# Neighbourhood attention: the products with the values, once 128 weight columns for a query group at a time, now 64 weight columns for one head, by key block

## The chip, the cores and the metric

The kernel runs on one core of one Trainium2 chip. The metric is the device time of one execution, in microseconds (us); before the change its median over three runs is 1502.55 us (1501.95 to 1504.43).

## The reference

One encoder layer over 1024 tokens of width 1024: a hybrid token mixer (an mLSTM group and a neighbourhood-attention group), cross-attention into 256 memory tokens, and a gated convolutional FFN, each followed by a layer norm. The change touches the neighbourhood attention alone. The tokens form a grid of 16 rows by 64 columns. Each of 8 heads of width 64 lets a token look at a window of 8 rows by 16 columns:

```python
s = jnp.einsum('bhrqd,bhrkd->bhrqk', qg, k_rows) * (NA_DIM ** -0.5)
s = jnp.where(mask, s + bias, -jnp.inf)
p = jax.nn.softmax(s, axis=-1)
o = jnp.einsum('bhrqk,bhrkd->bhrqd', p, v_rows)
```

`k_rows` and `v_rows` are the 8 grid rows that belong to a query row, `bias` is a learned relative bias, `mask` keeps the 16 columns. What changes is how the last line, the product of the probabilities with the values, is cut into matmuls.

## The kernel before

**Blocks.** `na_gen` (L1136) loops over four head pairs `p` and four column blocks `cb` of 16 query columns; such a pair is called a block here, and there are 16. The keys of a block lie in 32 columns of all 16 grid rows, 512 keys, which `vt` (L1175, three buffers, four loads of 64 KB on SyncE's queue) holds as four key blocks of 128 keys (4 grid rows by 32 columns), each with 128 value columns: 64 of the first head and 64 of the second. The queries of a block form four groups `g` of 4 grid rows. A group holds 64 queries of each head, side by side: 128 columns, the first 64 of head 0, the others of head 1. The groups see the key blocks 0-1, 0-2, 1-3 and 2-3, so 2, 3, 3 and 2 of them, 10 in all.

**A group's steps** (L1181 to L1205): scores `S` on TensorE by three matmuls in float32r (`mm3`, L224 to L226, into one of three "Y" banks of PSUM); VectorE adds bias and mask and takes the extreme (L1189); ScalarE the exponential with its sum (L1191); VectorE the reciprocal and the scaling (L1193, L1194). Then TensorE transposes the probabilities, one 128x128 transpose a key block (L1199, tile `tp`), ScalarE copies them to `PT` (L1201), and TensorE multiplies, in fp32, one matmul a key block:

```python
for b in range(nb):
    anchor[0] = T.matmul(po[:, g, :], vt[:, r0 // 4 + b, :], PT[:, b, :], start=b == 0,
                         stop=b == nb - 1)
```

The weights are all 128 value columns, the moving side all 128 queries, so the 128x128 result in `po` (tile `o`, one bank of the two "X" banks a block) holds each head's values under each head's queries. Only the two squares where the heads agree are used: after the fourth group, ScalarE and VectorE read them and split them into a high and a low part, `X2h` and `X2l` (L1206 to L1211, through `split`, L229 and L230).

**The order.** The program is written down group by group, and a scheduler then orders each engine's instructions by a timeline that it simulates, so what stands next to each other on an engine is not what the code says. `mix` (L30) adds a second product to the stage: `out_a` (L1219), the first half of the mixer's output projection (tile `fill`, bias added on GpSimd at L1094), of which it releases a part whenever the main generator has yielded enough of its total, 128 for 16 blocks of four groups with two yields each. After the last part, the weights of the second half of the projection (`w_mix_out`) are loaded; its matmuls (tile `out`, again L224 to L226) read `X2h` and `X2l` of all four head pairs, so those for the first three can run before the last head pair is done. The bias row `b_xo` of the next stage is scaled on VectorE at L1437.

Some small steps early in the program use only a part of the array: L377 multiplies with a single weight column, L385 transposes into 64 columns, L418 to L420 have one row, L431 transposes from 64 rows.

Of the kernel before, what the change touches and what calls it, by code (L numbers as in the profile page):

```python
# [8 lines left out]
F32 = mybir.dt.float32  # L9
# [4 lines left out]
AF = mybir.ActivationFunctionType  # L14
# [15 lines left out]
def mix(tc, anchor, main, total, fill, ftotal, lag, start=None):  # L30


    done = fdone = 0.0
    anchor[0] = start
    names = []
    more = True
    for cost in main:
        done += cost
        names.append(anchor[0])
        at = names[-1 - lag] if len(names) > lag else None  # L40
        while more and fdone / ftotal < done / total and at is not None:
# [15 lines left out]
def encoder(ctx, tc, I, out):  # L57
    nc = tc.nc
    V, A, G, T, S = nc.vector, nc.scalar, nc.gpsimd, nc.tensor, nc.sync
    anchor = [None]  # L60

    def bcast_row(ap, n, off=0):
# [10 lines left out]

    NB = {"X": 2, "Y": 3, "Z": 1, "tp": 2}
    SET = dict(tk="XXYYYZ", cl="X", xk="X", xv="X", st="X", stb="Y", s="Y", mem="XXYYYZ", cu="XXYYYZ", G="Z", num="Y", o="X", S="Y", xq="X", pv="X", S2="XXYYYZ",
               fill="Z", fill2="ZX", out="XXYYYZ", z="XXYYYZ", mx=["tp"], dn=["tp", "tp", "X", "X", "Y", "Y", "Y", "Z"])
# [151 lines left out]
    def split(hi, lo, src):  # L228
        A.activation(hi, src, AF.Copy)  # L229
        V.tensor_tensor(lo, src, hi.bitcast(F32), OP.subtract)  # L230
# [50 lines left out]
    with ExitStack() as ca:  # L281

        yml = None
        with ExitStack() as cm:
# [258 lines left out]
            with ExitStack() as c2:  # L543
# [12 lines left out]
                with ExitStack() as c1:  # L556
# [111 lines left out]
                    p0, s0 = pow2(ln_bound(lnw, lnb)[1], 12)  # L668
# [271 lines left out]
            wc, cb = {}, {}  # L940
# [160 lines left out]
        yna = tuple(t.rearrange("p (k t) -> p k t", k=4) for t in slot("X2"))  # L1101

        with ExitStack() as cn:
# [4 lines left out]
            o = 0  # L1108
# [23 lines left out]
                e_.memset(b_.bitcast(F32), 0.0)  # L1132
            CB = [0, 8, 24, 32]
            vload = [None]

            def na_gen():  # L1136
                n = 0
                for p in range(4):
                    if p % 2:
                        wide = wide1  # L1140
                    else:
                        wide = vecs.tile([128, D], F32, name="vec1", tag="vec1")[:, :576].rearrange(
                            "p (r c) -> p r c", r=12)
                    S.dma_start(wide, I["na_wide"][p])
                    if p == 0:
                        qr = vecs.tile([128, D], F32, name="vec2", tag="vec2").rearrange("p (r c) -> p r c", c=64)
                        kr = wp.tile([128, WP], F32, name="wraw", tag="wraw", bufs=2)[:, :D].rearrange(
                            "p (r c) -> p r c", c=64)
                    else:
                        qr = nw.tile([128, 16, 64], F32, name="qr", tag="qr", bufs=2)  # L1150
                        kr = nw.tile([128, 16, 64], F32, name="kr", tag="kr", bufs=2)
                    S.dma_start(qr, nqk_d[p].rearrange("p (r c) -> p r c", c=64))
                    S.dma_start(kr, nqk_d[4 + p].rearrange("p (r c) -> p r c", c=64))
                    for cb in range(4):
                        ct = (0, 1, 1, 2)[cb]
                        k0 = CB[cb]
                        if cb != 2:
                            for rt, R, dk0 in ((0, 8, 4), (1, 12, 0), (3, 8, 0)):
                                tb = tabs[ct, rt]
                                x0 = (16, 8, 0)[ct]  # L1160
                                G.tensor_tensor(tb, mo_[ct, R], wide[:, dk0:dk0 + R, x0:x0 + 32], OP.subtract)
# [12 lines left out]
                        (V if n < 2 else G).tensor_tensor(kl, kr[:, :, k0:k0 + 32], kh.bitcast(F32), OP.subtract)  # L1174
                        vt = nw.tile([128, 4, 128], F32, name="vt", tag="vt", bufs=3)  # L1175
                        for g in range(4):
                            vload[0] = S.dma_start(vt[:, g, :],
                                        bass.AP(tensor=nv_d.tensor, offset=nv_d.offset + (g * 256 + k0) * 512 + p * 128,
                                                ap=[[64 * 512, 4], [512, 32], [1, 128]]))
                        po = bank("o").rearrange("p (g t) -> p g t", g=4)  # L1180
                        for g in range(4):  # L1181
                            r0, R, rt = ((0, 8, 0), (0, 12, 1), (4, 12, 1), (8, 8, 3))[g]
                            nk = R * 32
                            ps = bank("S")[:, :nk]
                            mm3(ps, qh[:, g, :], ql[:, g, :], kh[:, r0:r0 + R, :].rearrange("p r c -> p (r c)"),
                                kl[:, r0:r0 + R, :].rearrange("p r c -> p (r c)"), True, True)
                            P = nw.tile([128, 384], F32, name="P", tag="P", bufs=5)
                            mn = nw.tile([128, 2], F32, name="mn", bufs=6)
                            V.tensor_tensor_reduce(P[:, :nk], ps, tabs[ct, rt].rearrange("p r c -> p (r c)"), 1.0, BIG,  # L1189
                                                   OP.add, OP.min, mn[:, 0:1])  # L1190
                            A.activation(P[:, :nk], P[:, :nk], AF.Exp, scale=-1.0, bias=mn[:, 0:1],  # L1191
                                         accum_out=mn[:, 1:2])
                            V.reciprocal(mn[:, 1:2], mn[:, 1:2])  # L1193
                            V.tensor_scalar(P[:, :nk], P[:, :nk], mn[:, 1:2], None, op0=OP.mult)  # L1194
                            yield 1
                            nb = R // 4
                            pt = tbank()
                            for b in range(nb):
                                T.transpose(pt[:, b, :], P[:, b * 128:(b + 1) * 128], ident)  # L1199
                            PT = nw.tile([128, 3, 128], F32, name="PT", tag="PT", bufs=3)  # L1200
                            A.activation(PT[:, :nb, :], pt[:, :nb, :], AF.Copy)  # L1201
                            for b in range(nb):
                                anchor[0] = T.matmul(po[:, g, :], vt[:, r0 // 4 + b, :], PT[:, b, :], start=b == 0,
                                                     stop=b == nb - 1)
                            yield 1  # L1205
                        for h in range(2):  # L1206
                            hs = slice(h * 64, h * 64 + 64)
                            src = po[hs, :, h * 64:h * 64 + 64].rearrange("p g (r c) -> p g r c", c=16)
                            oh, ol = (y[hs, p, :].rearrange("p (g r c) -> p g r c", r=4, c=64)
                                      [:, :, :, cb * 16:cb * 16 + 16] for y in yna)  # L1210
                            split(oh, ol, src)  # L1211
# [13 lines left out]
            oa = out_a()  # L1225
            S.dma_start(bmo, bcast_row(I["b_mix_out"], D))
            for _ in range(5):
                next(oa)
            mix(tc, anchor, na_gen(), 128.0, oa, 15.0, 1)

# [704 lines left out]
```

## Time and profile before

| what | value |
|---|---|
| median of three runs | 1502.55 us |
| the profiled execution | 1502.08 us |
| its span, first to last instruction | 1500.0 us |
| mean granted TensorE clock | 0.992 |
| TensorE busy with matmuls, whole span | 1441.3 us (96%) |
| first and last product with the values | 487.2 and 629.3 us |

A row of a timeline has the start, the duration, the engine, the line, the operation, what it writes and reads, its shape and how many; a wait in brackets is the idle time of the engine ahead of it and what ended it, "issue" meaning that the profile shows nothing that it waited for. PE stands for TensorE's matmuls, PEld for its weight loads, which run beside matmuls. An fp32 matmul leaves two records of each. A matmul's record begins when it is taken up and lasts until its result is written, so the records of a stream overlap, and a matmul's share of the engine is read from the distance of starts. Idle time of an engine other than the bound costs nothing.

### The profile page before, as it was taken

Reading aid. Unit: us, or ns where it says so; the run is one execution under the profiler, and the core shown is the slowest. Engines: PE = TensorE matmul, PEld = TensorE weight load, DVE = VectorE, ACT = ScalarE, POOL = GpSimd, SP = SyncE. Lnnn points to the kernel's source line nnn. Section 1 sums busy time; section 2 is a strip of 40 time slices with the busy share of each in tenths; the row PEclk is TensorE's granted clock in tenths of the full one; section 3 lists DMA queues with packets and bytes.
Section 4 is the critical chain, followed back from the end, with each engine's and each line's share of the span. In section 5 each row is a group of like instructions: output and inputs, shape, how many; then the busy total and the mean of one; then the engine's idle time right before and its main releaser. Section 6 shows DMA issues by size and latency. Waiting matters only on the chain. (4 is left out here: it accounts for less than half of the span.)

```text
span 1500.0 us, 21659 instructions
## 1 busy us (share of the span) xinstructions
PE 1441.3 (96%) x8060; PEld 867.1 (58%) x8060; DVE 1036.0 (69%) x1945; ACT 825.7 (55%) x1393; POOL 575.1 (38%) x453
## 2 busy tenths in 40 slices
PE   8999999999999898999999799999999999999998
PEld 6998866456766887874444344444444444444444
DVE  7867866545777687488555868887787789707424
ACT  5766565655554666425444777787777767503000
POOL 5452357303325766045112454443444320300543
PEclk9999999999999999999999899999999999999999
DMA  8846653215544633644333233232233336713121
GB/s 308 318 163 215 197 186 129 84 49 151 164 124 156 206 127 127 239 155 71 85 71 100 88 138 126 113 126 113 113 118 119 143 114 239 271 36 99 48 76 59
DMA packets 116383, 208.61 MB, mean 139 GB/s; under 512 B 40627, under 2 KB 69555, under 8 KB 112950
## 3 DMA queue, kind: packets, MB, share of 16 engines
q1 hardware_dynamic: 115984, 206.47, 41.3%
q8 instruction: 63, 1.03, 0.3%
q0 software_dynamic: 144, 0.49, 0.2%
q14 instruction: 42, 0.34, 0.1%
q10 hardware_dynamic: 150, 0.27, 0.0%
HBM read 154.15 MB, written 45.15 MB: 133 GB/s over the span
## 5 line engine op out<-in xcount | busy, mean ns | idle before, releaser
L1527 POOL TENSOR_TENSOR wraw<-ur 128x512 f32<-128x512 f32 x22 | 45.9, 2085 | 207.1 <-issue 192.3
L225 PE MATMUL dn<-wlo,yp 128*128 128x512 f16 (+1 forms) x284 | 105.1, 370 | 0.0
L224 PE MATMUL dn<-whi,yp 128*128 128x512 f16 (+1 forms) x284 | 104.9, 370 | 0.0
L226 PE MATMUL dn<-whi,yp 128*128 128x512 f16 (+1 forms) x284 | 104.4, 370 | 0.0
L1615 DVE SCALAR_TENSOR_TENSOR cbuf<-C,wdw,cbuf 128x1024 f32<-128x1024 f32 x44 | 69.8, 1587 | 35.0 <-ACT cbuf L1614 34.8
L226 PEld LDWEIGHTS <-wlo 128*128 128x128 f16 x540 | 52.8, 98 | 56.5 <-DVE wlo L204 1.3
L225 PEld LDWEIGHTS <-whi 128*128 128x128 f16 x540 | 52.8, 98 | 55.9 <-issue 3.3
L224 PEld LDWEIGHTS <-whi 128*128 128x128 f16 x540 | 52.8, 98 | 53.1 <-ACT whi L203 0.3
L242 POOL TENSOR_TENSOR lnrs<-lnrs,mhalf 128x1 f32<-128x1 f32 x32 | 25.9, 809 | 137.9 <-DVE lnrs L241 132.2
L204 DVE SCALAR_TENSOR_TENSOR wlo<-wraw,us,whi 128x1024 f16<-128x1024 f32 (+1 forms) x48 | 62.5, 1320 | 18.7 <-ACT whi L203 18.7
L1616 DVE SCALAR_TENSOR_TENSOR cbuf<-C,wdw,cbuf 128x1024 f32<-128x1024 f32 x44 | 70.4, 1601 | 0.7
L252 ACT ACTIVATE r<-r,lnrs 128x1024 f32<-128x1024 f32 x19 | 23.6, 1239 | 78.3 <-DVE lnrs L251 78.0
L203 ACT ACTIVATE whi<-wraw,us 128x1024 f16<-128x1024 f32 (+1 forms) x48 | 51.2, 1102 | 16.4 <-DVE us L176 15.5
L225 PEld LDWEIGHTS <-yp 128*128 128x128 f16 x370 | 36.2, 98 | 39.9
L224 PEld LDWEIGHTS <-yp 128*128 128x128 f16 x370 | 36.2, 98 | 39.8
L1614 ACT ACTIVATE cbuf<-C,bdw,wdw 128x1024 f32<-128x1024 f32 x44 | 54.2, 1234 | 9.1 <-DVE C L1652 8.5
L226 PEld LDWEIGHTS <-yp 128*128 128x128 f16 x370 | 36.2, 98 | 39.7
L224 PE MATMUL tk<-whi,Bo 128*128 128x256 f16 (+1 forms) x192 | 52.6, 274 | 2.5 <-DVE stage L204 2.5
L224 PE MATMUL tk<-whi,Be 128*128 128x256 f16 (+1 forms) x192 | 52.6, 274 | 0.7 <-DVE stage L204 0.7
L225 PE MATMUL tk<-wlo,Be 128*128 128x256 f16 (+1 forms) x192 | 52.4, 274 | 0.8 <-DVE wlo L204 0.8
L225 PE MATMUL tk<-wlo,Bo 128*128 128x256 f16 (+1 forms) x192 | 52.5, 274 | 0.0
L226 PE MATMUL tk<-whi,Be 128*128 128x256 f16 (+1 forms) x192 | 52.5, 274 | 0.0
(526 smaller groups left out, 4892.1 us busy)
## 6 DMA issues: line engine op xcount, KB each, us to landing
ur<-in_w_up_dram SPq DMA_DIRECT2D x22, 1024.0 KB
sv<-in_w_down_dram SPq DMA_DIRECT2D x22, 512.0 KB
y<-cbuf SPq DMA_DIRECT2D x22, 512.0 KB
ur<-y SPq DMA_DIRECT2D x11, 1024.0 KB
wraw<-in_w_down_dram SPq DMA_DIRECT2D x22, 512.0 KB
r<-h SPq DMA_DIRECT2D x11, 512.0 KB
wraw<-in_w_tok_dram SPq DMA_DIRECT2D x10, 512.0 KB
wr<-in_w_xk_dram SPq DMA_DIRECT2D x8, 512.0 KB
```

Of the source, the lines that this page charges most:

```text
L203: A.activation(hi, src, AF.Copy, scale=s)
L204: return V.scalar_tensor_tensor(lo, src, s, hi, op0=OP.mult, op1=OP.subtract)
L224: T.matmul(ps, lh, rh, start=first, stop=False, skip_group_check=skip)
L225: T.matmul(ps, lh, rl, start=False, stop=False, skip_group_check=skip)
L226: return T.matmul(ps, ll, rh, start=False, stop=last, skip_group_check=skip)
L242: G.tensor_tensor(rs[:, 0:1], rs[:, 0:1], mhalf[:, 0:1], OP.pow)
L252: A.activation(r, r, AF.Identity, scale=rs[:, 0:1], bias=rs[:, 1:2])
L1527: G.tensor_tensor(S1, A21, A22, OP.add)
L1614: A.activation(c, C[:, 1:SEQ + 1], AF.Identity, scale=wdw[:, 1, j:j + 1], bias=bdw[:, j:j + 1])
L1615: V.scalar_tensor_tensor(c, C[:, 0:SEQ], wdw[:, 0, j:j + 1], c, op0=OP.mult, op1=OP.add)
L1616: V.scalar_tensor_tensor(c, C[:, 2:SEQ + 2], wdw[:, 2, j:j + 1], c, op0=OP.mult, op1=OP.add)
```

## The change

- A new generator `pv_gen` makes the products of a block. It goes by key block: key block 0 meets groups 0 and 1, key blocks 1 and 2 three groups each, key block 3 groups 2 and 3 (`BG`). For each it issues two matmuls, one a head: 64 weight columns, the head's, into the head's half of the output partitions, and two or three groups of 64 queries as one moving side of 128 or 192 columns. That is 8 matmuls a block for 10, 128 for 160, and only the squares that are used are computed. The moving columns come to 20480 in both.
- So that the groups of a key block lie evenly spaced, `PT` becomes one tile of ten slots a block (two buffers in place of three single ones), sorted by key block (`GSLOT`).
- The products of a block are held in `late` and are issued during the next block: one key block after each group's copy to `PT`. The last block's products come at the end.
- A group now yields once, and the total that `mix` is given falls from 128 to 64.

```diff
+            GSLOT = (0, 1, 4, 7)
+            BG = ((0, 0, 2), (2, 0, 3), (5, 1, 4), (8, 2, 4))
+
+            def pv_gen(p, cb, vt, PT):
+
+                po = bank("o").rearrange("p (g t) -> p g t", g=4)
+                for b in range(4):
+                    s0, g0, g1 = BG[b]
+                    for h in range(2):
+                        hs = slice(h * 64, h * 64 + 64)
+                        anchor[0] = T.matmul(po[hs, g0:g1, hs], vt[:, b, hs], PT[:, s0:s0 + g1 - g0, hs], start=b == 0,
+                                             stop=b == 3, skip_group_check=True)
+                    yield 1
+                for h in range(2):
+                    hs = slice(h * 64, h * 64 + 64)
+                    src = po[hs, :, hs].rearrange("p g (r c) -> p g r c", c=16)
...
+                    split(oh, ol, src)
...
-                        po = bank("o").rearrange("p (g t) -> p g t", g=4)
+                        PT = nw.tile([128, 10, 128], F32, name="PT", tag="PT", bufs=2)
...
-                            PT = nw.tile([128, 3, 128], F32, name="PT", tag="PT", bufs=3)
-                            A.activation(PT[:, :nb, :], pt[:, :nb, :], AF.Copy)
-                            for b in range(nb):
-                                anchor[0] = T.matmul(po[:, g, :], vt[:, r0 // 4 + b, :], PT[:, b, :], start=b == 0,
-                                                     stop=b == nb - 1)
-                            yield 1
...
+                            A.activation(PT[:, GSLOT[g]:GSLOT[g] + 2 * nb - 1:2], pt[:, :nb, :], AF.Copy)
+                            if late is not None:
+                                next(late)
+                        if late is not None:
+                            run(late)
+                        late = pv_gen(p, cb, vt, PT)
+                yield 0
+                run(late)
...
-            mix(tc, anchor, na_gen(), 128.0, oa, 15.0, 1)
+            mix(tc, anchor, na_gen(), 64.0, oa, 15.0, 1)
```

How the instructions then stand, at three places. First TensorE in the middle of the stage, before: `o` are the products, `tp` the transposes, `S` the scores.

```order
L1203 MATMUL o<-PT,vt 128x128 x3
L1199 MATMUL tp<-ident,P 128x128 x2
L224 MATMUL S<-kh,qsh_5431 128x384
L225 MATMUL S<-kl,qsh_5431 128x384
L226 MATMUL S<-kh,qsl_5432 128x384
L224 MATMUL S<-kh,qsh_5431 128x256
L225 MATMUL S<-kl,qsh_5431 128x256
L226 MATMUL S<-kh,qsl_5432 128x256
L1203 MATMUL o<-PT,vt 128x128 x2
L1199 MATMUL tp<-ident,P 128x128 x3
L1203 MATMUL o<-PT,vt 128x128 x2
L1199 MATMUL tp<-ident,P 128x128 x3
```

And after, about the same place:

```order
L1219 MATMUL tp<-ident,P 128x128 x2
L1145 MATMUL o<-PT,vt 64x3x64 x2
L1219 MATMUL tp<-ident,P 128x128 x3
L1145 MATMUL o<-PT,vt 64x3x64 x2
L1145 MATMUL o<-PT,vt 64x2x64 x2
L224 MATMUL S<-kh,qsh_5431 128x256
L225 MATMUL S<-kl,qsh_5431 128x256
L226 MATMUL S<-kh,qsl_5432 128x256
L1219 MATMUL tp<-ident,P 128x128 x3
L224 MATMUL S<-kh,qsh_5440 128x256
L225 MATMUL S<-kl,qsh_5440 128x256
L226 MATMUL S<-kh,qsl_5441 128x256
```

Before, the stage has 64 stretches of products, one a group; after, the 64 pairs (one a key block) stand in 46 stretches, mostly three a block, the last two key blocks of a block together.

The second place is TensorE at the end of the stage, before (`out` is the second half of the output projection):

```order
L1203 MATMUL o<-PT,vt 128x128 x3
L224 MATMUL out<-whi,X2h 128x512
L225 MATMUL out<-wlo,X2h 128x512
L226 MATMUL out<-whi,X2l 128x512
L224 MATMUL out<-whi,X2h 128x512
L225 MATMUL out<-wlo,X2h 128x512
L226 MATMUL out<-whi,X2l 128x512
L224 MATMUL out<-whi,X2h 128x512
L225 MATMUL out<-wlo,X2h 128x512
L226 MATMUL out<-whi,X2l 128x512
L1203 MATMUL o<-PT,vt 128x128 x2
L224 MATMUL out<-whi,X2h 128x512
```

And after:

```order
L1219 MATMUL tp<-ident,P 128x128 x3
L1145 MATMUL o<-PT,vt 64x3x64 x2
L1145 MATMUL o<-PT,vt 64x2x64 x2
L1219 MATMUL tp<-ident,P 128x128 x3
L1219 MATMUL tp<-ident,P 128x128 x2
L1145 MATMUL o<-PT,vt 64x2x64 x2
L1145 MATMUL o<-PT,vt 64x3x64 x4
L1145 MATMUL o<-PT,vt 64x2x64 x2
L224 MATMUL out<-whi,X2h 128x512
L225 MATMUL out<-wlo,X2h 128x512
L226 MATMUL out<-whi,X2l 128x512
L224 MATMUL out<-whi,X2h 128x512
```

Before, the last product is followed at once by output matmuls of the last head pair, which need its split; after, the last block's eight products stand together behind the last transposes, and nine output matmuls of the first three head pairs come behind them.

The third place is VectorE where it scales `b_xo`, before (`ISA` is the reduction with bias and mask, `mn` its extreme and the reciprocal):

```order
L1193 RECIPROCAL mn<-mn 128x1
L1189 ISA P,mn<-S,tb_1_5434 128x384
L1189 ISA mn 128x1
L230 TENSOR_TENSOR X2l<-o,X2h 64x16x16
L1194 TENSOR_SCALAR P<-P,mn 128x256
L1437 TENSOR_SCALAR vec_7270<-vec_7270 128x1024
L1193 RECIPROCAL mn<-mn 128x1 x2
L1194 TENSOR_SCALAR P<-P,mn 128x256
```

And after, where L1437 has become L1453:

```order
L1209 ISA P,mn<-S,tb_1_5434 128x384
L1209 ISA mn 128x1
L230 TENSOR_TENSOR X2l<-o,X2h 64x16x16
L1213 RECIPROCAL mn<-mn 128x1
L1453 TENSOR_SCALAR vec_7190<-vec_7190 128x1024
L1214 TENSOR_SCALAR P<-P,mn 128x256
L1213 RECIPROCAL mn<-mn 128x1
L230 TENSOR_TENSOR X2l<-o,X2h 64x16x16
```

It stands behind the same reduction, with the softmax of the same groups behind it. On SyncE's queue the loads of `w_mix_out` for the second half stand four value loads later than before. Behind the attention stage the cross-attention is in the same order; in the FFN some 30 short pieces have changed places.

More of the change, by code (lines that the diff above doesn't have):

```diff
@@ L75, in encoder @@
     SET = dict(tk="XXYYYZ", cl="X", xk="X", xv="X", st="X", stb="Y", s="Y", mem="XXYYYZ", cu="XXYYYZ", G="Z", num="Y", o="X", S="Y", xq="X", pv="X", S2="XXYYYZ",
-               fill="Z", fill2="ZX", out="XXYYYZ", z="XXYYYZ", mx=["tp"], dn=["tp", "tp", "X", "X", "Y", "Y", "Y", "Z"])
+               fill="Z", out="XXYYYZ", z="XXYYYZ", mx=["tp"], dn=["tp", "tp", "X", "X", "Y", "Y", "Y", "Z"])
     turn = {}
@@ L1134, in encoder @@
             vload = [None]
+            GSLOT = (0, 1, 4, 7)
[12 more added lines that the diff above has]
+                    src = po[hs, :, hs].rearrange("p g (r c) -> p g r c", c=16)
+                    oh, ol = (y[hs, p, :].rearrange("p (g r c) -> p g r c", r=4, c=64)
+                              [:, :, :, cb * 16:cb * 16 + 16] for y in yna)
+                    split(oh, ol, src)
             def na_gen():
+                late = None
                 n = 0
@@ L1199, in na_gen @@
                                 T.transpose(pt[:, b, :], P[:, b * 128:(b + 1) * 128], ident)
-                            PT = nw.tile([128, 3, 128], F32, name="PT", tag="PT", bufs=3)
-                            A.activation(PT[:, :nb, :], pt[:, :nb, :], AF.Copy)
-                            for b in range(nb):
-                                anchor[0] = T.matmul(po[:, g, :], vt[:, r0 // 4 + b, :], PT[:, b, :], start=b == 0,
-                                                     stop=b == nb - 1)
-                            yield 1
[L1206 to L1211, printed above, removed]
+                            A.activation(PT[:, GSLOT[g]:GSLOT[g] + 2 * nb - 1:2], pt[:, :nb, :], AF.Copy)
[6 more added lines that the diff above has]
+                run(late)
             def ylk(y):
```

## The prediction, on record before the run

> **What bounds the kernel now.** I read the page first, then the windows over the neighbourhood-attention stage, then who waited for whom there, then the instructions one by one. The page says that TensorE is the busy engine of the whole program:
>
> ```profile
> PE 1441.3 (96%) x8060; PEld 867.1 (58%) x8060; DVE 1036.0 (69%) x1945; ACT 825.7 (55%) x1393; POOL 575.1 (38%) x453
> ```
>
> That is an average over stages, so the stage itself decides. The products with the values run from 487 to 629 us. Columns: stretch, its length, busy time of each engine (instructions), granted clock, DMA share, GB/s.
>
> ```profile
> 500.00:510.00 10.00, 5.46 (x29) 5.01 (x28) 6.79 (x21) 3.42 (x11) 5.88 (x6) 0.83 0.44 136
> 510.00:540.00 30.00, 30.00 (x208) 27.82 (x207) 23.60 (x66) 21.47 (x62) 21.92 (x24) 1.00 0.48 154
> 540.00:580.00 40.00, 37.34 (x247) 33.15 (x246) 30.55 (x95) 27.34 (x81) 27.57 (x27) 1.00 0.30 99
> 580.00:610.00 30.00, 24.30 (x150) 21.58 (x149) 25.64 (x63) 19.31 (x51) 14.81 (x12) 0.94 0.53 177
> ```
>
> From 510 to 580 PE is busy 67.3 of 70 us and DVE 54.2: a microsecond more or less of TensorE work there is a microsecond of the stage. The holes are at 500 to 510 and 580 to 610. The waits of PE in 476 to 632, and one of DVE (total, times, longest):
>
> ```profile
> PE S L224 <- DVE mn L1189: 8.8, 6, 4.5
> PE o L1203 <- ACT PT L1201: 2.4, 3, 1.9
> PE out L224 <- ACT X2h L229: 1.3, 1, 1.3
> DVE vec L1437 <- DMA vec<-in_b_xo_dram: 4.6, 1, 4.6
> ```
>
> The longest hole is DVE standing 4.6 us for a bias row of the next stage, with the softmax behind it. The change leaves that instruction where it is (one row later on DVE, behind the same reduction), so this hole stays in my sum. The products themselves wait for their probabilities only 2.4 us in all.
>
> **The products: how many columns.** This is the PE timeline (start, duration, line, tile, times) of one query group with three key blocks:
>
> ```profile
> 514.03 0.28 PE L225 MATMUL S<-kl,qsh 128*128 128x256 f32 x1
> 514.15 0.28 PE L226 MATMUL S<-kh,qsl 128*128 128x256 f32 x1
> 514.27 0.83 PE L1203 MATMUL o<-PT,vt 128*128 128x128 f32 x6
> 514.93 0.38 PE L1199 MATMUL tp<-ident,P 128*128 128x128 f32 x2
> ```
>
> Durations overlap, starts don't: six records of L1203 take 514.93 - 514.27 = 0.66 us, 0.11 each. A product is two records (160 in the program, 320 here), so before they cost 320 x 0.11 = 35.2 us:
>
> ```profile
> L1203 PE MATMUL o<-PT,vt 128*128 128x128 f32 x320 | 48.0, 282 | 2.5 <-ACT PT L1201 2.4
> L1201 ACT ACTIVATE PT<-tp 128x384 f32<-128x384 f32 x32 | 15.3, 480 | 6.7 <-PE tp L1199 6.5
> ```
>
> After, each of the 16 blocks (head pair, column block) has four key blocks with 2, 3, 3 and 2 query groups of 64 columns, for each of two heads: eight matmuls of two records, 128 or 192 columns long. By the row above a record of 128 columns takes 0.11, one of 192 then 0.11 x 1.5 = 0.165. One after the other that is 8 x 0.11 + 8 x 0.165 = 2.2 us a block, 35.2 us in all: nothing is saved, since the columns are the same 20480. A saving exists only where the two heads, which sit in different halves of the array, stream side by side. No row of before has two such matmuls next to each other, so I bound it. Lower end: 35.2. The records stand as head 0 first, head 0 second, head 1 first, head 1 second; the second record of a head needs the same half as its first, so in a lone pair only the two in the middle can overlap: three record times for four. In the order a block mostly makes three unbroken stretches, of one, one and two pairs: 3 x 0.11 + 3 x 0.165 + (3 x 0.165 + 2 x 0.11) = 1.54 us, 24.6 in all, 10.6 saved. If whole pairs overlapped it would be 17.6. I take 10.6: the pair's operands share neither weight columns nor output partitions, and the order of the records forbids more.
>
> **What it adds: the array changes its division.** Everything around these products fills all 128 columns. Before has a few places where a smaller tile stands between full ones, and there the weight loads (PEld) show what happens:
>
> ```profile
> 190.68 0.27 PE L225 MATMUL tk<-wlo,Bo 128*128 128x256 f16 x1
> 190.79 0.27 PE L226 MATMUL tk<-whi,Bo 128*128 128x256 f16 x1
> ```
>
> ```profile
> 190.68 0.10 PEld L226 LDWEIGHTS <-Bo 128*128 128x128 f16 x1
> 190.99 0.14 PEld L431 LDWEIGHTS s<-ident,Mr 64*128 64x128 f32 x1 [0.21 <-issue]
> 191.19 0.10 PEld L224 LDWEIGHTS <-Bo 128*128 128x128 f16 x1
> ```
>
> The last full matmul starts at 190.79 and, at 0.11 each, its columns are through at 190.90; the next load, with nothing to wait for, starts at 190.99: 0.09 us in which the array empties, and the load can't hide behind a matmul as others do. For columns in place of rows there is one place, 32 wide:
>
> ```profile
> 131.33 0.30 PEld L376 LDWEIGHTS s<-lf,triL 128*128 128x128 f32 x2
> 131.67 0.09 PEld L377 LDWEIGHTS s<-lf,ones 128*1 128x1 f32 x2
> 131.87 0.10 PEld L224 LDWEIGHTS <-whi 128*128 128x128 f16 x1
> ```
>
> Loads of L376 are 0.11 apart, the second is in at 131.55, its 32 columns take 0.03; the load of L377 starts at 131.67: 0.09 again. Its two records of 64 columns (0.055 each) are through at 131.78, and the full load behind starts at 131.87: 0.09 on the way back too. The exposed loads: of two L420 loads (64 columns) in 0.19 us each lasts 0.13, so they are 0.06 apart; full ones in fp32 are 0.30 - 0.19 = 0.11 apart.
>
> ```profile
> 176.24 0.30 PEld L419 LDWEIGHTS s<-rows,ones 1*128 1x128 f32 x2
> 176.60 0.19 PEld L420 LDWEIGHTS s<-ones,rows 1*64 1x64 f32 x2
> L420 PEld LDWEIGHTS s<-ones,rows x2: 128/130/131, 176.6 to 176.7; 1*64 1x64 f32 x2
> L419 PEld LDWEIGHTS s<-rows,ones x2: 187/187/187, 176.2 to 176.3; 1*128 1x128 f32 x2
> ```
>
> So a stretch of products costs 0.09 + 0.06 going in and 0.09 + 0.11 coming out, 0.35 us. The changed order has the 64 pairs in 46 unbroken stretches: 46 x 0.35 = 16.1 us. The Trainium skill says the same of such changes (TensorEngine Tiling (Array Packing), Tiling Modes: changing the mode, not just the tile, drains the engine); by that rule, and by the rows alike, it speaks against this change. One row speaks the other way, a transpose into 64 columns with no gap at all:
>
> ```profile
> 144.77 0.10 PEld L226 LDWEIGHTS <-Bo 128*128 128x128 f16 x1
> 144.88 0.11 PEld L385 LDWEIGHTS s<-ident,g_sb 128*64 128x64 f32 x1
> 144.99 0.10 PEld L224 LDWEIGHTS <-Be 128*128 128x128 f16 x1
> ```
>
> It is a transpose and the new products are none, so I lean on L377; but it is the only 64-column row, and I keep it as a rival. The same page (Restrictions) says that column tiling and fp32 transposes exclude each other; by that L385 was never a column tile, and the gap would come.
>
> **The rest, and the sum.** The products now trail their block by one: they no longer follow the copy of their own probabilities, so the 2.4 us of waiting for ACT go (bound: 0 to 2.4; I take all, since a whole block lies between). At the end nine output matmuls now stand between the last products and the first one that needs the X2 split, so 1.3 us go; but all eight last products wait for the last copy, 0.48 by its row: -0.8. Of the 8.8 us in which PE waits for DVE, 4.5 belong to the bias row; of the other 4.3, where DVE is late, a slower PE gives some back: 0 to 4.3, I take 1.0, since 510 to 580 shows hardly any. Copies, softmax, splits and value loads are the same in number and size and run beside PE; GpSimd does the same steps in a slightly other order. The mix's total is halved with the number of yields, so the other product comes at the same pace; the second half of w_mix_out is loaded four value loads later, and 36 instead of 45 output matmuls come ahead of the last product, the rest behind it: the same work, so nothing.
> Sum on PE: -10.6 + 16.1 = +5.5; with -2.4 - 0.8 - 1.0 it is +1.3 us. The profiled execution took 1502.08 (span 1500.0), so 1503.4; the median of the three runs is 0.47 above it: 1503.9. A measurement of this kernel tells 0.2%, 3.0 us, from no change; the forecast is within that.
>
> **The rivals.** Each on the same base, 1502.55.
> - *Gaps, but no overlap* (slower). The heads stream one after the other: 0 saved, 16.1 added, 4.2 given back: +11.9, 1514.5. It decides as soon as overlap saves under 0.35 us a stretch; taken alone it means that the halves don't do what the change asks of them. For it: nothing in before shows two halves at once. Against: nothing forbids it.
> - *Overlap, no gaps* (faster). L385 is right for 64 columns: -10.6 - 2.4 - 0.8 = -13.8, 1488.8. DVE, at 54.2 of 70, would still follow.
> - *Neither*: 2.4 and 0.8 alone, 1499.4.
> - *Whole pairs overlap, with gaps*: -17.6 + 16.1 - 3.2 = -4.7, 1497.9. Against it: two records of a head need the same half. The Trainium skill (TensorE: Matmul & The Clock Gate, Part 3) gives for packed matmuls one duration and about 4 ns for each further tile, which would be this case if it held for two-record products.
>
> **How the numbers follow.** Forecast 0.54, no overlap 0.20, no gaps 0.15, neither 0.07, whole pairs 0.04. The forecast's own range is 1500 to 1508 (waits given back or not, a stretch at 0.30 to 0.36): of it 0.1 is faster by over 3.0 us, 0.55 the same, 0.35 slower. Faster: 0.05 + 0.15 + half of 0.07 + most of 0.04 = 0.27; slower: 0.19 + 0.20 = 0.39; the same: 0.34. The range takes in most of both large rivals: 1490 to 1513.
>
> **What would show it.** Right: in the changed profile the loads of head 0's first record start 0.09 us after the columns of the last full matmul, and those of the full matmul behind likewise; the first record of head 1 starts within 0.02 us of head 0's second; PE's waits for the PT copy are gone; the DVE hole at the bias row is still there. Wrong: head 1's records start a record time (0.11 or 0.165) apart from head 0's second (no overlap), or no gap at the edges of a stretch, or new waits of PE that no term here names.

## The result and the profile after

The changed kernel takes 1491.66 us (median of 4 runs, 1489.96 to 1492.36), the kernel before took 1503.49 beside it (4 runs, 1501.95 to 1505.74). The ratio is 0.9918, 95% interval [0.9901, 0.9936]: faster by 0.8%, where I had forecast no measurable change. The profiled executions took 1502.08 and 1489.96 us, 12.12 apart. Of all executions told here one, of the experiment e7 below, was slow (1860.12 us, the other three of e7 1488.97 to 1489.78); its ratio leaves it out.

The page of after, busy time by engine (share of the span, instructions), in a span of 1488.2 us:

```profile
PE 1434.5 (96%) x7996; PEld 843.5 (57%) x7996; DVE 1032.6 (69%) x1945; ACT 823.8 (55%) x1393; POOL 574.8 (39%) x453
```

PE's share is what it was, and says nothing: it lost 6.8 us of busy time in a span that lost 11.8. The windows of after over the stage answer to those of before:

```profile
500.00:510.00 10.00, 5.23 (x22) 3.93 (x21) 5.61 (x14) 3.86 (x12) 5.98 (x6) 0.83 0.45 146
510.00:540.00 30.00, 30.00 (x192) 23.25 (x192) 22.91 (x71) 21.90 (x64) 22.13 (x24) 1.00 0.47 156
540.00:580.00 40.00, 39.28 (x259) 30.15 (x258) 32.13 (x101) 28.58 (x86) 29.84 (x33) 1.00 0.35 114
580.00:610.00 30.00, 25.50 (x160) 18.30 (x159) 26.18 (x78) 23.14 (x64) 13.18 (x9) 0.94 0.52 171
```

From 510 to 580 PE is busy 69.3 of 70 us by this view, so the product stretches look as dense as the rest. Their cost shows only one level lower. The PE timeline of after around one pair of 128-column products, then one of 192:

```profile
525.40 0.38 PE L1219 MATMUL tp<-ident,P 128*128 128x128 f32 x2
525.71 0.44 PE L1145 MATMUL o<-PT,vt 128*64 128x128 f32 x4
526.08 0.39 PE L225 MATMUL S<-kl,qsh 128*128 128x256 f32 x1
...
527.09 0.55 PE L1145 MATMUL o<-PT,vt 128*64 128x192 f32 x4
527.56 0.44 PE L224 MATMUL S<-kh,qsh 128*128 128x384 f32 x1
```

And its weight loads:

```profile
525.25 0.30 PEld L1219 LDWEIGHTS tp<-ident,P 128*128 128x128 f32 x2
525.71 0.20 PEld L1145 LDWEIGHTS o<-PT,vt 128*64 128x64 f32 x4 [0.17 <-issue]
526.08 0.19 PEld L225 LDWEIGHTS S<-kl,qsh 128*128 128x128 f32 x1 [0.17 <-issue]
```

The second transpose starts 0.11 behind the first, at 525.51, and is through at 525.62; the first half load starts at 525.71: 0.09 us of an empty array, as forecast. The next full load starts at 526.08, so the whole stretch of one pair took 0.37. That number decides: with the load of 64 columns (0.05) and the gap behind (0.09) it leaves 0.23 for the columns, two records of 0.11, where three would need 0.33 and four 0.44. Record by record, to the nanosecond, the trace has

```
525.713  head 0, first record      525.873  head 0, second record
525.720  head 1, first record      525.880  head 1, second record
```

Both records of a head run beside both of the other, 7 ns behind. The 192-column pair says the same: 527.56 - 527.09 = 0.47, against 0.05 + 2 x 0.16 + 0.09 = 0.46.

PE's waits in the stage, after:

```profile
PE fill L224 <- DVE r L1089: 5.6, 2, 4.8
PE S L224 <- DVE mn L1209: 2.5, 5, 0.7
PE tp L1219 <- DVE P L1214: 1.2, 1, 1.2
PE out L224 <- ACT whi L126: 1.1, 1, 1.1
PE out L224 <- DVE r L1091: 1.1, 1, 1.1
PE tp L1219 <- ACT PT L1220: 0.4, 1, 0.4
```

The products don't stand among them any more (before 2.4 for the copies of PT), the output matmuls no longer wait for the X2 split (1.3), the scores wait 2.5 in place of 8.8. The hole at the bias row is there as forecast; only another line of PE (`fill`, 4.8) now stands at its end, and behind the bias row DVE waits for one more transfer:

```profile
DVE vec L1453 <- DMA vec<-in_b_xo_dram: 3.7, 1, 3.7
DVE r L1089 <- DMA r<-h: 2.3, 1, 2.3
```

Where the 12.12 us went: the stage itself (first matmul of `fill` to last of `out`) fell from 195.6 to 186.4, -9.2. It began 0.9 later, the stretch from the last `out` to the first `z` is 0.9 shorter, the part from there to the last matmul 2.7 shorter, and 0.2 lie outside the span. For the stage I took each PE record's columns from the trace and added up the time between them, in us; *edges* are the pauses where the width of the weights changes, *long* the other pauses over 0.45, *short* those under it, *rest* all that is left, the other matmuls above all. The last four columns are experiments told below.

```
                    before   after     e1      e3      e9      e4      e12
products, columns    34.88   18.03   34.44   17.57   17.55   27.15   26.96
edges                 0      15.28    0       6.36    5.50    6.84    5.52
long pauses          20.57   16.53   17.90   23.83   17.19   15.21   13.82
short pauses          5.27    2.54    4.34    5.66    5.27    6.36    6.47
rest                134.86  134.02  134.08  134.02  134.11  134.17  134.24
stage               195.58  186.40  190.76  187.44  179.62  189.73  187.01
```

In the stage, then, the columns gave 16.9 and the edges took back 15.3; the pauses gave 6.8 (4.0 and 2.7). These figures come from one profiled execution of each kernel, and a single hole can differ between two of them by some 2 us that no edit touched (see e11).

### The profile page after: what moved, and what is told of

Read it like the earlier page. It is cut to its first block, busy times and chain, and to the rows that moved or that the text cites. A ratio compares the mean times of both kernels' runs of the same rounds, so it can differ in the third digit from the quotient of the medians.

```text
span 1488.2 us, 21528 instructions
## 1 busy us (share of the span) xinstructions
PE 1434.5 (96%) x7996; PEld 843.5 (57%) x7996; DVE 1032.6 (69%) x1945; ACT 823.8 (55%) x1393; POOL 574.8 (39%) x453
## 5 line engine op out<-in xcount | busy, mean ns | idle before, releaser
L224 PE MATMUL tk<-whi,Bo 128*128 128x256 f16 (+1 forms) x192 | 52.5, 274 | 2.3 <-DVE stage L204 2.3
L226 PE MATMUL tk<-whi,Bo 128*128 128x256 f16 (+1 forms) x192 | 52.5, 274 | 0.0
```

Source lines behind the costliest of these rows:

```text
L224: T.matmul(ps, lh, rh, start=first, stop=False, skip_group_check=skip)
L226: return T.matmul(ps, ll, rh, start=False, stop=last, skip_group_check=skip)
```

## The experiments

All are measured against the kernel before, in the same session on the same chip; kernels of different sessions are best compared by their ratios. The scheduler orders every kernel anew. Where an experiment only holds work back (e6 to e11), 98% or more of TensorE's instructions in the stage stand in the same order as in the kernel it is compared with; where it changes the products (e1 to e4, e12) or the release (e5), less, so there more differs than the edit says. My theory after the result: whole pairs overlap, the gaps cost what I said, and a part of the gain comes from the order of the work and not from the halves. The rivals: the halves give all of it, or the waits decide and neither the columns nor the gaps matter.

**Full width (e1).** The changed loop with all 128 weight columns in one matmul: by key block as in after, again 46 stretches, no halves. Its order is not that of after: set side by side, about a fifth of TensorE's instructions in the stage stand elsewhere.

```
-                    for h in range(2):
-                        hs = slice(h * 64, h * 64 + 64)
-                        anchor[0] = T.matmul(po[:, g0:g1, hs], vt[:, b, hs], PT[:, s0:s0 + g1 - g0, hs], start=b == 0,
-                                             stop=b == 3, skip_group_check=True)
+                    anchor[0] = T.matmul(po[:, g0:g1, :], vt[:, b, :], PT[:, s0:s0 + g1 - g0, :], start=b == 0,
+                                         stop=b == 3, skip_group_check=True)
```

> The changed kernel with full-width products: by key block and in the changed order as after, but one matmul of 128 weight columns and 256 or 384 moving columns instead of two of 64, so no half tiles and no change of the array's division. Theory A (the tiles give little: in the trace of after the products' columns fall from 34.9 to 18.0 us, but 46 stretches pay about 0.33 us each at their edges, 15.3; the rest of the 12 us comes from the order, by fewer waits): about 1.5 us slower than after, near 1493 to 1495, with waits as in after. Rival B (the tiles give the gain): back to before, 1500 to 1504.

Measured: 1495.15 against 1502.85, ratio 0.9951 [0.9933, 0.9968]. Its products take the 34.4 us of before and there are no edges, and yet over half of the gain is there. The stage is 4.8 shorter, 3.6 of it in the pauses. PE's waits of e1, to be set beside the 8.8 + 2.4 + 1.3 of before:

```profile
PE S L224 <- DVE mn L1207: 5.4, 5, 1.8
PE tp L1217 <- DVE P L1212: 4.2, 1, 4.2
PE out L224 <- ACT whi L126: 1.9, 2, 1.2
```

From e1 to after the ratio falls from 0.9951 to 0.9918, about 5 us (3.5 by the medians); the intervals just touch, but the stage says the same (190.8 to 186.4). Of these 4.4 us, the columns less the edges make 1.1 (16.4 against 15.3) and shorter pauses 3.2. Whether the halves or the other order shortened the pauses, no run shows.

**Products of the own block (e2).** The products follow their own probabilities again, in place of standing a block behind in the program.

```
-                            if late is not None:
+                            if g == 0:
+                                late = pv_gen(p, cb, vt, PT)
+                            else:
                                 next(late)
-                        if late is not None:
-                            run(late)
-                        late = pv_gen(p, cb, vt, PT)
-                yield 0
-                run(late)
+                        run(late)
```

> The changed kernel without the delay by a block: the products of a key block are written down right after the groups it needs, in their own block. Theory A (the gain beside the tiles comes from the key-block form and the order, and the scheduler hoists the delayed products to where their probabilities are ready anyway): within 3 us of after, 1489 to 1495. Rival C (the delay is what removes the waits on TensorE): 5 to 8 us slower than after, 1496 to 1500, with TensorE waiting for ScalarE's copies again.

Measured: 1493.81, ratio 0.9944 [0.9927, 0.996]; the interval touches that of after. PE waits for the copies again, less than before:

```profile
PE S L224 <- DVE mn L1209: 8.4, 5, 6.0
...
PE o L1145 <- ACT PT L1220: 1.7, 4, 0.8
```

Theory A came out: the delay is worth 1.7 us of that wait and little else that the runs show. The stage, 187.0, is 0.6 longer than after's, in 48 stretches for 46. What more there is in the profiled execution (1.0 between the last `out` and the first `z`, 1.9 behind) lies where the order is the same, so the trace doesn't put it down to the delay.

**One stretch a block (e3).** All eight products stand together behind the transposes of the next block's second group: 16 stretches in place of 46, which saves 9 us of edges if PE is what counts.

```
-                                T.transpose(pt[:, b, :], P[:, b * 128:(b + 1) * 128], ident)
+                                lt = T.transpose(pt[:, b, :], P[:, b * 128:(b + 1) * 128], ident)
-                            if late is not None:
-                                next(late)
-                        if late is not None:
-                            run(late)
+                            if late is not None and g == 1:
+                                with tc.issue_after(lt.ins):
+                                    run(late)
```

> The changed kernel with all eight products of a block issued together, behind the transposes of the next block's second group: 16 stretches instead of 46. Theory A (each stretch costs 0.33 us of TensorE time on the path): 30 x 0.33 = 9.9 us faster than after if nothing else comes late, 1481 to 1486 with some waiting for VectorE given back. Rival D (the gaps fall into time in which TensorE would wait for the softmax anyway): within 3 us of after.

Measured: 1490.02, ratio 0.9915 [0.99, 0.993], the same as after. Rival D came out. The edges did fall by 8.9; the pauses rose by 10.4. PE's timeline of e3 shows where most of that is:

```profile
592.67 0.44 PE L1219 MATMUL tp<-ident,P 128*128 128x128 f32 x2 [0.17 <-ACT PT L1220]
599.16 0.69 PE L224 MATMUL S<-kh,qsh 128*128 128x384 f32 x1 [6.05 <-DVE mn L1209]
```

The next scores wait 6.05 us for DVE. DVE's own timeline there (the bracket is its idle time and what ended it):

```profile
593.42 1.22 DVE L196 TENSOR_REDUCE sc<-vec 128x1 f32<-128x1024 f32 x1 [1.90 <-DMA vec<-in_ln_w_dram]
594.67 0.43 DVE L230 TENSOR_TENSOR X2l<-o,X2h 64x256 fp32r<-64x256 f32 x1
595.13 1.23 DVE L127 TENSOR_TENSOR wlo<-wraw,whi 128x1024 fp32r<-128x1024 f32 x1
596.27 2.30 DVE L199 SCALAR_TENSOR_TENSOR sc<-sc 128x1 f32<-128x1 f32 x1
598.49 0.15 DVE L1213 RECIPROCAL mn<-mn 128x1 f32<-128x1 f32 x1
598.67 0.42 DVE L1209 CUSTOM_DVE_ANT_0 P<-S,tb 128x256 f32<-128x256 f32 x1
```

VectorE stands 1.90 us for a weight row of the layer norm behind the stage and reduces it (L196); then come the attention's own split (L230), a split of output weights (L127) and the bound that is worked out from the row (L199), while the softmax waits behind in the queue. L199 works on a single column and lasts 2.30 us here. It ends 15 ns behind an operation of GpSimd that was under way when it started:

```profile
596.01 2.54 POOL L127 TENSOR_TENSOR wlo<-wraw,whi 128x1024 fp32r<-128x1024 f32 x1 [4.64 <-ACT whi L126]
```

It is the same in after, e1, e2, e5, e7 and e8: L199 starts beside a GpSimd operation and ends 13 to 18 ns behind it. In before, e4 and e9 to e12 none runs beside it, and it takes 0.14 to 0.15 us. So some 2 us of the hole are GpSimd's. e9 takes the hole up.

**Heads apart (e4).** As e3, but the four products of head 0 and then the four of head 1: few neighbours in different halves.

```
-                for b in range(4):
-                    s0, g0, g1 = BG[b]
-                    for h in range(2):
-                        hs = slice(h * 64, h * 64 + 64)
+                for h in range(2):
+                    hs = slice(h * 64, h * 64 + 64)
+                    for b in range(4):
+                        s0, g0, g1 = BG[b]
```

> As the kernel with 16 stretches, but a stretch holds the four products of head 0 and then the four of head 1, instead of the heads in turn. Theory A1 (each half of the array takes its own matmuls as soon as it is free, whatever stands between): the same as the kernel with 16 stretches. Theory A2 (matmuls start in the order of the program, and only neighbours in different halves overlap): the columns of a block take about 2.0 us instead of 1.1, 14 us more in all, so slower than the kernel with 16 stretches by 10 to 14 us.

Measured: 1492.16, ratio 0.9932 [0.9917, 0.9947]. A stretch of the same 16 records takes longer; the PE timelines of e4, and of e3 for comparison:

```profile
521.10 1.90 PE L1145 MATMUL o<-PT,vt 128*64 128x128 f32 x16
522.93 0.55 PE L1219 MATMUL tp<-ident,P 128*128 128x128 f32 x3
```

```profile
589.78 1.31 PE L1145 MATMUL o<-PT,vt 128*64 128x128 f32 x16
591.02 0.38 PE L224 MATMUL S<-kh,qsh 128*128 128x256 f32 x1
```

From the first record to the next full matmul it is 1.83 in place of 1.24. To the nanosecond, head 0's records start at 521.097, .257, .365, .529, .691, .854, 522.016 and .125, and head 1's first at 521.697, with head 0's third product: the second half starts two products ahead of its turn, not four. All products cost 27.2 us of columns against 17.6, so the halves overlap less than A1 says and more than A2. But these 9.6 us cost only 2.1 us of time by the medians, and the intervals overlap: in e3 something else than PE sets the pace for a good part.

**The FFN's order alone (e5).** The kernel before with one number changed, which gives TensorE the order in the FFN that it has after the change. In the attention stage the products stay as they were, in 64 stretches; some instructions change places there too, at about the same length (196.2 against 195.6).

```
-            mix(tc, anchor, na_gen(), 128.0, oa, 15.0, 1)
+            mix(tc, anchor, na_gen(), 128.0, oa, 15.0, 2)
```

> The kernel before, with one number changed: the other product is released one step later (a lag of 2 for 1). Its products with the values are those of before, in 64 stretches of full width; the order of the FFN comes out instruction for instruction as in after. Theory A (some 2.5 us of the gain are the FFN's order: TensorE waits less for VectorE's maxima there): the FFN takes 435 to 438 us in the profile as in after, not 439, the attention stage about 196, in all 1 to 4 us faster than before. Rival F (the FFN's difference is scatter between executions): the FFN at 439 and the time within 1 us of before.

Measured: 1499.76 (10 runs) against 1502.12 (19 runs), ratio 0.9985 [0.9975, 0.9994]. So about 2 us of the 12 come with the short pieces in the FFN that changed places. The traces agree: from the first `z` to the last matmul before takes 654.8 us, and the thirteen other kernels, which all have TensorE's order of after there, take 650.8 to 653.9. One line of the waits of PE behind the stage, in before, after and e5, shows a part of it:

```profile
PE mx L182 <- DVE am L1493: 5.7, 7, 1.8
```

```profile
PE mx L182 <- DVE am L1509: 2.5, 4, 1.6
```

```profile
PE mx L182 <- DVE am L1493: 3.7, 6, 1.5
```

**The bias row late (e6, e7, e8).** The scaling of `b_xo`, in front of which DVE stood 3.7 us, is held behind the last softmax scaling: in after (e6), in e3 (e7) and in e5 (e8). The edit in each, with `vsm[0]` the last softmax scaling:

```
-        V.tensor_scalar(bxo, bxo, 1.0 / ALPHA, None, op0=OP.mult)
+        with tc.issue_after(vsm[0].ins):
+            V.tensor_scalar(bxo, bxo, 1.0 / ALPHA, None, op0=OP.mult)
```

> The changed kernel with the scaling of the next stage's bias row on VectorE held behind the last softmax step, so that nothing on VectorE waits for that row's transfer in the middle of the stage. Theory A (after is bound by the softmax's chain as well as by TensorE, and the hole at 500 us stops both): 4 to 5 us faster than after, 1486 to 1488. Rival G (the transfers around 500 us hold the stage anyway, or the time is given back to other waits): within 2 us of after.

> The kernel with 16 stretches of products, with the bias row's scaling held back likewise. Theory A (without the hole TensorE is the bound again and the 9 us of gaps that 16 stretches save come through in part): 3 to 8 us faster than the changed kernel with the bias held back, 1479 to 1484. Rival D (the waits for the softmax take the place of the gaps, hole or no hole): the same as that kernel within 2 us.

> The kernel before with the later release (the FFN's order of after) and the bias row's scaling held back likewise. Theory A (the hole costs before as much as after): 4 to 5 us faster than the same kernel with the scaling where it was, 1494 to 1498. Rival G: within 2 us of it.

Measured: 0.992 [0.9903, 0.9936], 0.9913 [0.9896, 0.9929] and 0.9991 [0.9981, 1.0] (1490.1, 1489.62 and 1500.12 us against 1502.12): no gain that the intervals can tell in any, so rival G (in e7 D) came out each time. In e6 the wait for the bias is gone, and in its place DVE waits for the next transfer:

```profile
DVE r L1089 <- DMA r<-h: 5.4, 1, 5.4
```

So the largest single hole of the stage was not worth its length: another transfer was nearly as late. In the one execution of e6 that was profiled, the fastest of its four, the stage is 184.6, 1.8 shorter than in after; a gain of that size can't be excluded.

**The layer-norm bound late (e9, e10, e11).** The reductions of L196 and L197 and the bound of L199 are held there too: in e7 (e9), e6 (e10) and e8 (e11).

```
-            p1, s1 = pow2(ln_bound(lw, lb)[1], 14)
+            with tc.issue_after(vsm[0].ins):
+                p1, s1 = pow2(ln_bound(lw, lb)[1], 14)
```

> This is the kernel with all eight products of a block in one stretch and the scaling of b_xo held behind the last softmax scaling, and now the two reductions over ln1_w and ln1_b and the bound worked out from them are held there too. Theory F (the saved gaps are lost at one place: at 591 to 599 VectorE waits 1.7 us for the transfer of ln1_w and then does two reductions of 1.2 us each in front of the softmax, so that TensorE stands 5.3 us for the scaled scores' extremes at about 593): the hole of TensorE at 593 falls from over 5 us to under 3 us, the stage is 2 to 4 us shorter, and the ratio to before falls from 0.991 to 0.988 to 0.990. Theory H (the saved gaps are lost all along the stage, the softmax chain sets the pace, or the wait for the output weights behind it takes the place of the hole): the stage stays within 1 us of 188, the ratio 0.990 to 0.992, and the hole at 593 is still there with another name or is spread over several waits.

> The changed kernel (46 stretches) with the scaling of b_xo, the reductions over ln1_w and ln1_b and the bound from them all held behind the last softmax scaling. Theory F: here VectorE had no long wait at that place, only 2.4 us of reductions in front of the softmax, so at most 1 to 2 us go: 0.990 to 0.992, and less than with one stretch a block. Theory H: nothing, 0.991 to 0.993; the ranking of the two orders stays a tie.

> The kernel before with the FFN order of the changed one, the scaling of b_xo held behind the last softmax scaling, and now the reductions over ln1_w and ln1_b and their bound held there too. Theory F (holding the reductions back pays where the products have been gathered into one stretch a block, because only there has TensorE time to spare): at most 1.5 us below the same kernel without it (0.9991), 0.997 to 0.999. Rival (the reductions stand in the way of any order, the gain has nothing to do with the products): 5 to 7 us go here too, 0.994 to 0.996.

Measured: e9 1484.79 us (against 1502.62), ratio 0.987 [0.9849, 0.9891]; e10 1489.15, 0.9907 [0.989, 0.9923]; e11 1497.75 (against 1501.96), 0.9967 [0.9956, 0.9978]. e9 lies below the interval of after: it beats both kernels. The same place in e9, PE and then DVE:

```profile
592.36 0.44 PE L1220 MATMUL tp<-ident,P 128*128 128x128 f32 x2 [0.43 <-ACT PT L1221]
593.47 0.45 PE L224 MATMUL S<-kh,qsh 128*128 128x384 f32 x1 [0.67 <-DVE mn L1210]
```

```profile
591.14 1.74 DVE L127 TENSOR_TENSOR wlo<-wraw,whi 128x1024 fp32r<-128x1024 f32 x1
592.81 0.15 DVE L1214 RECIPROCAL mn<-mn 128x1 f32<-128x1 f32 x1
592.99 0.42 DVE L1210 CUSTOM_DVE_ANT_0 P<-S,tb 128x256 f32<-128x256 f32 x1
```

The softmax follows straight on, and the hole of 6.05 is 0.67. GpSimd's split now holds a softmax scaling instead (L1215 at 594.41, 2.43 us long, behind GpSimd's operation from 594.25 to 596.62), without a hole of PE. How much of the gain is the wait for the weight row and how much that L199 no longer stands beside GpSimd in front of the softmax, no run separates. The stage fell by 8.0 from e7's 187.65 to 179.63, at least twice what I had expected. In e10 the same edit gives no gain that the intervals can tell: with 46 stretches PE had only short waits at that place. e11 lands between the two expectations: 2.4 us below e8 by the medians (3.6 by the ratios, whose intervals don't touch), where e9 is 4.8 below e7 (6.5 by the ratios). Its stage is only 0.8 shorter (194.76 to 194.00), but DVE's wait for a transfer that the edit doesn't touch happens to be 1.8 longer in e11; here e8, then e11:

```profile
DVE r L1089 <- DMA r<-h: 2.7, 1, 2.7
```

```profile
DVE r L1089 <- DMA r<-h: 4.5, 1, 4.5
```

PE's wait at that place is 3.1 in e8 and 4.9 in e11. Without this the stage would be some 2.6 shorter (an estimate, 0.8 + 1.8), as the time is. So the reductions stood in the way of the old order too, and two to three times as much in the gathered one.

**Heads apart without that hole (e12).** e4 with the edits of e9.

> One stretch a block with four products of head 0 and then four of head 1 (little overlap, 9.6 us more of columns than with the heads by turns), with the scaling of b_xo and the reductions over ln1_w and ln1_b held behind the last softmax scaling. While the reductions stood in the way these 9.6 us cost 2.1 us. Theory F (with the hole gone TensorE sets the pace again): they cost 5 to 9 us now, the ratio is 0.990 to 0.993 against 0.987 with the heads by turns. Theory H (the softmax chain or the output weights still set the pace): at most 3 us, 0.987 to 0.989.

Measured: 1490.7, ratio 0.9922 [0.9909, 0.9934]. Against e9 the 9.4 us of columns that the missing overlap costs now cost 7.4 us of the stage and 5.9 of the time by the medians (7.8 by the ratios, whose intervals don't touch); with the hole the time had been 2.1. PE's waits in e12 are all short, so PE sets the pace again for the most part:

```profile
PE fill L224 <- DVE r L1089: 2.2, 2, 1.4
PE tp L1220 <- DVE P L1215: 1.4, 1, 1.4
PE tp L1220 <- ACT PT L1221: 1.3, 2, 1.0
PE tp L1220 <- DVE mn L1214: 1.3, 1, 1.3
```

## Why the prediction was wrong, by its own steps

- *The columns: 24.6 us after, 10.6 saved.* **This step failed.** It said that "the order of the records forbids more" than the middle two of a lone pair. The trace shows each half of the array taking its own head's records, two beside two: 18.0 us, 16.9 saved. e4 and e12 confirm that this is overlap of neighbours: with the heads apart, 27.2 and 27.0. It is the rival "whole pairs overlap, with gaps", to which I had given 0.04. The 4 ns for each further tile that the Trainium skill (TensorE: Matmul & The Clock Gate, Part 3) states, and that I cited beside that rival, do hold for two-record products, nearly: 7 ns here. I let an argument about the order of records outweigh it, and no row of before spoke to either.
- *The gaps: 46 x 0.35 = 16.1.* Right: 15.3, or 0.33 a stretch, with 0.09 of drain both ways. The rows of three small tiles elsewhere in before had carried the whole price. The rule of the Trainium skill (TensorEngine Tiling (Array Packing), Tiling Modes) is that a change of the mode drains the array. This trace agrees, with 0.09 us at each edge; that the transpose of L385 shows no gap did not carry over to these products.
- *The waits: -2.4, -0.8, -1.0.* The first is right by its row (2.4 to 0), though not by its reason: the scheduler pulls the first pair of a block forward to just behind its own block's last transposes, and the other pairs follow the next block's first two groups, so no whole block lies between. The other two were too small: long pauses fell by 4.0 and short ones by 2.7, where the three terms make 4.2. e1 shows 3.6 of it without halves. I had taken 1.0 of the 4.3 us in which scores wait for DVE because I expected a PE no faster than before.
- *Everything outside the stage: no term.* Wrong by 2.9. I had seen that short pieces of the FFN change places and gave that no price; e5 gives it 2.3 us, interval 0.9 to 3.8. The 0.9 between attention and FFN is not the change's: that stretch takes 171.4 or 172.3 in kernels that agree in its order.
- *The sum.* +1.3 against -12.1: 6.3 from the columns, 0.8 from the edges, 2.6 from the pauses, 0.8 from the rest of the stage, 2.9 from outside. The rival with whole pairs was at 1497.9, six too high, because it shared the misses behind the columns. That 1491.66 lies inside the stated 1490 to 1513 is luck: the lower end was there for the rival without gaps, and the gaps are there.
- *That PE's microsecond is the stage's microsecond.* In the changed kernels it holds only in part; no run tests it on before. e3 saved 9 us of PE and gained nothing, e4 added 9.6 and lost 2.1; once DVE's layer-norm work is out of the way 9.4 cost 5.9 to 7.8 (e12).

Open: why the pauses shrink by 6.8, of which e1 has over half without halves, the order being new in each kernel; why GpSimd's operation holds L199 and the softmax scalings and not every VectorE instruction; and what e9's gain is made of.

## What to carry to other kernels

Price a division of the array by two numbers: what a pair saves (half its columns, if the two halves stand next to each other in the program) and what a stretch costs (0.33 us here), and gather the pairs until the first is well above the second. When that saves less than it should, look at what stands in front of the softmax in VectorE's queue: here work for the next stage stood there, waiting first for a late transfer and then for GpSimd. With it the gathering gained nothing, and holding it back was worth 5 us. A hole that is named after one transfer can have a second transfer behind it (e6), so removing it is an experiment and no forecast.

## What the runs showed of the hardware

- Two fp32 products of two records each, in the two column halves, run as whole pairs: second starts 7 ns behind first, for the first records and the second (525.713 and .720, 525.873 and .880).
- The loads of the two halves start 7 ns apart (525.711 and 525.718), and the second load of head 0 starts at 525.766, with the first records of both heads under way since 525.713 and 525.720.
- The overlap reaches only near neighbours here: in e4, with four products of each half in a row, the other half starts two products before its turn.
- From the end of full-width columns to the first half load, and from the end of half columns to the next full load, 0.09 us each, in 46 stretches as in 16 (15.3 / 46 = 0.33 and, in e9 and e12, 5.5 / 16 = 0.34 us with the exposed loads; the same division gives 0.40 in e3 and 0.43 in e4, where one stretch each holds a delay of 0.9 and 1.3 us besides).
- A VectorE instruction that starts beside a GpSimd operation can last until that is through, however short it is itself: L199 as told under e3, and in after the 37 softmax scalings that start beside one, which end 0.15 to 0.35 us behind it and take up to 2.57 us, while the 27 others take 0.34 to 0.42. The reciprocals are not held: none in after takes more than 0.17.
